# A two-layer mixer and MoE decoder: layer change interleaved, last sum kept in PSUM, branch hints near the branch

## The chip, the core and the metric

The kernel runs as one program on one core of a Trainium2 chip. The metric is device time of one execution in microseconds. Engines are named as in the profile: PE is TensorE (PEld its weight loads), DVE VectorE, ACT ScalarE, POOL GpSimd, SP the engine whose queue issues the transfers.

## What is computed

```python
for l in range(2):                                   # 256 tokens, width 1024
    h = layer_norm(ALPHA * h + mixer(h), ln1_g[l], ln1_b[l])
    h = layer_norm(ALPHA * h + moe(h),   ln2_g[l], ln2_b[l])

def layer_norm(x, g, b):
    mu = mean(x); var = mean((x - mu) ** 2)
    return (x - mu) * rsqrt(var + 1e-5) * g + b

def moe(h):                                          # 16 experts, top 2 of one group of 4
    for e in range(16):
        y += combine[:, e] * ((silu(h @ w1[e]) * (h @ w3[e])) @ w2[e])   # 1024 -> 512 -> 1024
```

The mixer begins with one wide projection of `h`, whose columns feed three attention branches.

## The kernel before

Every weight streams from HBM once, in pieces of 1 MB, over SP's queue into a ring of tiles (`ST`, issues at L96 and L100). A tile goes back to the ring when its last matmul is done, and the next piece is issued into it. float32 products of the mixer are made from two halves: ACT rounds a tile (`whi`, L370), DVE subtracts to get the rest (`wlo`, L371), and PE multiplies high by high, low by high and high by low (L375 to L377).

**MoE.** Eight pairs of experts p follow each other in an order written by hand (`block` ties each step on PE to the step before). `up` (L1557) multiplies the gathered tokens by w1 and w3, `down` (L1600) by w2. `down`'s 128x512 results are split by ACT into `yh` (L1609) and by DVE into `yl` (L1610), and `combine` adds them, weighted and scattered back to the tokens, into four accumulators in PSUM, which stay open over all eight pairs (`z` in layer 0 at L1515, `ya` in layer 1 at L1520). After p = 3 stands a branch (`overflow`, L1453): experts with more than 64 tokens would be finished in a loop. The inputs give none, so every engine jumps over that code; in the program's order it lies between p = 3 and p = 4. Each engine takes this branch on its own. A hint for it exists for PE alone, and lies right at the start of the program and right behind the first branch.

**Layer change.** The second norm of layer 0 is not finished before layer 1's first projection (the q columns) begins. `finish` (L1528) adds the residual to the accumulators (`zf`, L1539), `raw_split` (L297 on ACT, L298 on DVE) splits each eighth of it into high and low, and PE multiplies these raw sums by q's weights (L964); mean and scale are put right later. The first half of q's weight is split at L949 (ACT) and L950 (DVE) into `gl`. `norm` transposes `zf` on PE (L934), takes the statistics on DVE (L935), scales into `r`, and PE transposes `r` (L319) for the second projection (`kv`).

**End.** In layer 1 `finish` adds the residual to `ya` and writes the sum back to SBUF (`r`, L1532), then takes statistics from it (L1533). For the last pair's second column half (`down(7)`, c = 1) the work goes in two parts of 256 columns, and the last weight piece is loaded in two halves to suit. The last norm runs on DVE in two steps for each of three 512-column pieces (L1673: minus mean, times gain; L1674: times scale, plus bias), and for two 256-column pieces on ACT (L1667) and POOL (L1669, L1670). Each piece goes out by a transfer of its own (L1675).

Of the kernel before, what the change touches and what calls it, by code (L numbers as in the profile page):

```python
# [9 lines left out]
F32 = mybir.dt.float32  # L10
F32R = mybir.dt.float32r
# [58 lines left out]
def trunk(ctx, tc, x, consts, pcol, rowv, gb, wfm, wng, wdv, wmla, wcmp, wcmp2, wu, wbr, wout, rw, mw1, mw3, mw2, out):  # L70
# [223 lines left out]
    def raw_split(ps, i, k, z):  # L294
        g = ln_cols(i, k)[0]
        hi, lo = [v[:, 0:S] for v in z[k]]
        X0["z", k] = A.activation(hi, ps, AF.Copy, scale=g).ins  # L297
        V.scalar_tensor_tensor(lo, ps, g, hi.bitcast(F32), op0=ALU.mult, op1=ALU.subtract)  # L298

    def raw_fix(rs, nbs, psp, bc):  # L300
# [42 lines left out]
    def mixer(l, res, z, zf):  # L343
# [577 lines left out]

        def norm():
            r, i = res, 2 * l
            pool, tag = ST.take()
            if zf is None:
                rs, nbs, X["norm"] = ln_norm2(r, [ln_stats(r, t) for t in range(2)])
            else:
                zt = [[p.tile([P, 512], F32, name=n) for c in range(2)] for p, n in ((pO, "o"), (pS, "s"))]
                sts = [sm.tile([P, 2, 6], F32, name="lnst") for t in range(2)]
                for c in range(2):  # L930
                    for t in range(2):
                        for k in range(4):
                            with tc.issue_after(X["raw", 0, 0]):
                                T.transpose(zt[t][c][:, k * P:k * P + P], zf[:, 4 * c + k, t * P:t * P + P], ident)  # L934
                        V.bn_stats(sts[t][:, c], zt[t][c])  # L935
                rs, nbs, X["norm"] = ln_norm2(r, sts, zt)
            bc = pool.tile([P, 2048], F32, name="bc", tag=tag)
            psps = [(pT, "pt"), (pT, "pt"), (pO, "o"), (pO, "o"), (pS, "s")]
            xT[:] = ln_split_T(r, i, X["evq"], psps, *(ST.take() if zf is None else X0["zf"]))
            with tc.issue_after(X["evq"]):  # L940
                raw_fix(rs, nbs, pS, bc)
            return bc
# [1 line left out]
        add_fm("kv", xT, 4, ev1)  # L944
        add_tm("ng", xT, 280, ev2)
        w = wtile("q", 0, KD, 256)
        gl = mg.tile([P, 2, 4, 256], F32R, name="gl", tag="gt0")
        with tc.issue_after(X0["z", 1 if "yh" in X0 else 3]):
            i = A.copy(gl[:, 0], w[:, 0:4])  # L949
        V.tensor_sub(gl[:, 1], w[:, 0:4], gl[:, 0].bitcast(F32))  # L950
        with tc.issue_after(i.ins):
            w0 = [(gl[:, 0], gl[:, 1]), split(w[:, 4:8], [P, 4, 256], mb, OHL[1][1])]
        with tc.issue_after(i.ins):
            for c in fq[2:4]:
                c.h = c.prep()
            gbt = load_gb(mh, 2 * l, "gt1", nc.scalar)
# [377 lines left out]
    def moe(l, R):  # L1334
# [164 lines left out]
        def wg(*key):  # L1499
            key = (l,) + key  # L1500
            return ST.get(key), lambda: ST.done(key)
# [25 lines left out]
        def finish(c, ks):  # L1527
            if last:  # L1528
                for t in range(2):
                    a, b = ks[0] * P, ks[1] * P  # L1530
                    d = res[:, t, 512 * c + a:512 * c + b]
                    V.scalar_tensor_tensor(d, d, ALPHA, ya[t][c][:, a:b], op0=ALU.mult, op1=ALU.add)  # L1532
                    V.bn_stats(sts[t][:, c + ks[0] // 2], d)  # L1533
                return
            if c == 0:
                Z["z"] = raw_tiles(2 + 2 * l)
            for j in range(2 * c + ks[0] // 2, 2 * c + ks[1] // 2):
                d = Z["zf"][:, 2 * j:2 * j + 2]
                X0["zf", j] = V.tensor_add(d, ya[j], d).ins  # L1539
            for k in range(4 * c + ks[0], 4 * c + ks[1]):  # L1540
                raw_split(Z["zf"][:, k], 2 + 2 * l, k, Z["z"])

# [45 lines left out]
        def down(p):  # L1588
            gT = gTs[p]
            Y[p] = []  # L1590
            for c in range(2):
                parts = ((0, 2), (2, 4)) if (p, c) == (7, 1) else ((0, 4),)
                ye = [pf.tile([P, (b - a) * P], F32, name="pt") for a, b in parts]
                for h in range(2):
                    w2t, fin = wg("w2", 2 * p + c, h)
                    for v, ks in zip(ye, parts):
                        for f in range(2):
                            for j in range(2):
                                c0 = (2 * f + j) * 512
                                i = T.matmul(v[64 * j:64 * j + 64], gT[:, 2 * h + f, 64 * j:64 * j + 64],  # L1600
                                             w2t[:, c0 + ks[0] * P:c0 + ks[1] * P],
                                             start=(h == 0 and f == 0), stop=(h == 1 and f == 1), skip_group_check=True)
                    fin()
                yh = gp.tile([P, 512], F32R, name="yh")
                yl = gp.tile([P, 512], F32R, name="yl")
                Y[p].append((yh, yl))
                for v, ks in zip(ye, parts):
                    d = slice(ks[0] * P, ks[1] * P)
                    X0["yh"] = A.copy(yh[:, d], v).ins  # L1609
                    V.tensor_sub(yl[:, d], v, yh[:, d].bitcast(F32))  # L1610
                for ks in parts if p == 7 else ():
                    combine(7, c, ks)
                    finish(c, ks)
            return i

        for p in range(8):
            hs = [pf.tile([P, FF], F32, name="pt") for _ in range(2)]
            for nm, hh in zip(("w1", "w3"), hs):
                block(up, p, nm, hh)
            if p == 0:  # L1620
                lent.close()
                mx.append(right.enter_context(tc.tile_pool(name="mx2", bufs=1, side="right", reuse_waits="tile")))
                gp = right.enter_context(tc.tile_pool(name="gp", bufs=2, side="right", reuse_waits="tile"))
                block(slot_weights, 0)
            g = hidden(p, *hs)
            if p in (0, 4):
                block(gather, p // 2 + 1)
                block(slot_weights, p // 2 + 1)
                block(slots_T, p)
                block(turn, p, g)  # L1630
                if p == 4 and last:
                    affine()
                continue
            block(down, p - 1)
            block(turn, p, g)
            block(slots_T, p)
            if p == 2:
                block(gather, 2)
                block(slot_weights, 2)
            if p == 7 and not last:  # L1640
                pool, tag = X0["zf"] = ST.take()
                Z["zf"] = pool.tile([P, KD, S], F32, name="zf", tag=tag)
                for k in range(KD):
                    block(residual, k)
            for c in range(2):
                block(combine, p - 1, c)
            if p == 3:
                tc.mark_branch_hint_location('ov', 'LikelyTaken', engines=[mybir.EngineType.PE])
            if p in (3, 7):
                block(down, p)  # L1650
            if p == 3:
                for c in range(2):
                    block(combine, 3, c)
                overflow()
                PEQ.clear()
        r = res if last else hp.tile([P, 2, D], F32, name="r", tag="r")
        if last:
            gbt = [mx[b].tile([P, D], F32, name="gb", tag=f"xe{b}") for b in (2, 0)]
            for j, v in enumerate(gbt):
                nc.sync.dma_start(v, bass.AP(tensor=gb.tensor, offset=gb.offset + (4 + 4 * l + j) * D, ap=[[0, P], [1, D]]))  # L1660
            mr, nbs, ins = ln_mr2(sts)
            for t, a, b in ((1, 512, 768), (1, 768, 1024), (0, 0, 512), (0, 512, 1024), (1, 0, 512)):
                mu, rs = mr[t]
                d = r[:, t, a:b]
                g, bb = [v[:, a:b] for v in gbt]
                if b - a < 512:
                    A.activation(d, d, AF.Identity, bias=nbs[t], scale=rs)  # L1667
                    with tc.issue_after(i) if a > 512 else nullcontext():
                        G.tensor_mul(d, d, g)  # L1669
                    i = G.tensor_add(d, d, bb).ins  # L1670
                else:
                    with tc.issue_after(ins):
                        V.scalar_tensor_tensor(d, d, mu, g, op0=ALU.subtract, op1=ALU.mult)  # L1673
                    ins = V.scalar_tensor_tensor(d, d, rs, bb, op0=ALU.mult, op1=ALU.add).ins  # L1674
                nc.sync.dma_start(out[t * P:(t + 1) * P, a:b], d)  # L1675
        right.close()
        RBS.close()
# [153 lines left out]
```

## Time and profile before

| what | value |
|---|---|
| median of 3 runs | 1046.31 us (1044.56, 1046.31, 1046.35) |
| profiled execution | 1044.16 us |
| its span, first to last instruction | 1042.5 us |
| mean granted TensorE clock | 0.989 |
| PE busy | 1005.7 us (96%) |
| DVE, ACT, POOL busy | 533.7, 423.7, 31.7 us |
| bytes moved | 294.88 MB, 283 GB/s on average |

The span is what the trace shows; 1.7 us lie outside it. All times in the rows are microseconds from the span's start. PE is busy nearly all the time, so a gain has to come from the places where it waits or runs at a low clock.

### The profile page before, as it was taken

The numbers are of one execution on the slowest core, as the hardware profiler recorded it, in microseconds if no ns is written. First come the engines' busy times: TensorE is split into PE (matmuls) and PEld (weight loads), VectorE is DVE, ScalarE is ACT, GpSimd is POOL, SyncE is SP. The second block draws the span as 40 slices with busy tenths as digits, with TensorE's granted clock in tenths as the row PEclk, the third lists the DMA queues.
The fourth block names the chain that finished last, engine by engine and source line by source line (L and its number), as shares of the span: only waits on it lengthen the run. The fifth ranks groups of instructions, "written<-read, shape, count | busy, mean of one in ns | idle before, by whom it ended". The sixth has DMA issues, their size and how long they took to land. (4 is left out here: it accounts for less than half of the span.)

```text
span 1042.5 us, 16792 instructions
## 1 busy us (share of the span) xinstructions
PE 1005.7 (96%) x6498; PEld 707.3 (68%) x6498; DVE 533.7 (51%) x1493; ACT 423.7 (41%) x991; POOL 31.7 (3%) x46
## 2 busy tenths in 40 slices
PE   8999999999989999999899999999999999989994
PEld 7888888999864344433597888799998544424332
DVE  7755778785772121211395558777777422102315
ACT  6564677564432121211455547755553221101110
POOL 0300000000000000000001001000000000000001
PEclk8999999999999999999999999999999999999998
DMA  9664334548867999999955544345497789999993
GB/s 358 250 243 137 138 122 164 182 141 345 321 258 302 422 420 420 420 421 420 389 182 215 188 152 155 130 146 177 158 374 300 290 321 422 421 418 421 420 421 133
DMA packets 45543, 294.88 MB, mean 283 GB/s; under 512 B 5136, under 2 KB 7952, under 8 KB 11792
## 3 DMA queue, kind: packets, MB, share of 16 engines
q1 hardware_dynamic: 44880, 291.51, 71.3%
q10 hardware_dynamic: 576, 2.24, 0.5%
q8 instruction: 51, 0.84, 0.3%
q14 instruction: 36, 0.29, 0.1%
HBM read 292.68 MB, written 1.05 MB: 282 GB/s over the span
## 5 line engine op out<-in xcount | busy, mean ns | idle before, releaser
L1557 PE MATMUL pt<-wt,xe 128*64 128x512 f32 x1024 | 226.3, 598 | 5.3 <-DVEq L1453 4.7
L371 DVE TENSOR_TENSOR wlo<-wt,whi 128x1024 fp32r<-128x1024 f32 (+4 forms) x146 | 167.4, 1148 | 81.9 <-ACT whi L370 75.7
L370 ACT CAST whi<-wt 128x1024 fp32r<-128x1024 f32 (+4 forms) x146 | 143.8, 987 | 147.1 <-PE acc L376 103.5
L1557 PEld LDWEIGHTS pt<-wt,xe 128*64 128x64 f32 x1024 | 72.9, 138 | 143.9 <-issue 133.7
L375 PE MATMUL acc<-hi,whi 128*128 128x256 f32 x576 | 165.4, 289 | 1.7 <-ACT whi L370 0.8
L377 PE MATMUL acc<-hi,wlo 128*128 128x256 f32 x576 | 164.0, 286 | 0.8 <-DVE wlo L371 0.8
L376 PE MATMUL acc<-lo,whi 128*128 128x256 f32 x576 | 162.3, 282 | 0.0
L1600 PE MATMUL pt<-wt,gT 128*64 128x512 f32 (+1 forms) x544 | 113.9, 568 | 0.0
L375 PEld LDWEIGHTS acc<-hi,whi 128*128 128x128 f32 x576 | 108.1, 188 | 7.9 <-issue 3.9
L377 PEld LDWEIGHTS acc<-hi,wlo 128*128 128x128 f32 x576 | 108.3, 188 | 4.2 <-DVE wlo L371 2.1
L376 PEld LDWEIGHTS acc<-lo,whi 128*128 128x128 f32 x576 | 108.7, 189 | 0.3 <-DVE lo L339 0.2
L1609 ACT CAST yh<-pt 128x512 fp32r<-128x512 f32 (+1 forms) x34 | 19.1, 560 | 184.2 <-PE pt L1600 184.2
L1600 PEld LDWEIGHTS pt<-wt,gT 128*64 128x64 f32 x544 | 38.7, 137 | 70.6 <-issue 65.8
L1610 DVE TENSOR_TENSOR yl<-pt,yh 128x512 fp32r<-128x512 f32 (+1 forms) x34 | 22.4, 659 | 106.0 <-ACT yh L1609 106.0
L1568 DVE SCALAR_TENSOR_TENSOR g<-g,pt 128x512 f32<-128x512 f32 x16 | 11.0, 686 | 126.6 <-ACT g L1567 126.6
L1567 ACT ACTIVATE g<-pt 128x512 f32<-128x512 f32 x16 | 9.6, 597 | 120.4 <-PE pt L1557 120.4
L375 PE MATMUL acc<-ob,whi 128*128 128x256 f32 x192 | 56.8, 296 | 1.1 <-DVE gt L892 0.8
L376 PE MATMUL acc<-ob,whi 128*128 128x256 f32 x192 | 54.2, 282 | 0.0
L377 PE MATMUL acc<-ob,wlo 128*128 128x256 f32 x192 | 54.2, 284 | 0.0
L1569 DVE SCALAR_TENSOR_TENSOR g<-g,wsl,pt 128x512 f32<-128x512 f32 x16 | 11.9, 746 | 69.0 <-PE pt L1557 69.0
L659 DVE COPY ts<-pt 128x384 f32<-128x384 f32 x56 | 30.5, 551 | 30.7 <-PE pt L628 30.6
L1382 ACT ACTIVATE xe<-pt,pc 128x128 f32<-128x128 f32 x60 | 24.2, 453 | 53.3 <-PE pt L1324 51.6
(399 smaller groups left out, 1763.1 us busy)
## 6 DMA issues: line engine op xcount, KB each, us to landing
wt<-in_mw SPq DMA_DIRECT2D x190, 1024.0 KB, 16.8
wt<-in_wfm SPq DMA_DIRECT2D x38, 1024.0 KB, 4.9
wt<-in_wbr SPq DMA_DIRECT2D x12, 1024.0 KB, 4.8
wt<-in_wcmp SPq DMA_DIRECT2D x8, 1024.0 KB, 6.2
wt<-in_wout SPq DMA_DIRECT2D x8, 1024.0 KB, 8.1
wt<-in_wdv SPq DMA_DIRECT2D x4, 1024.0 KB, 6.2
wt<-in_wmla SPq DMA_DIRECT2D x4, 832.0 KB, 5.8
wt<-in_wng SPq DMA_DIRECT2D x4, 560.0 KB, 12.8
```

What stands on the lines that cost most here:

```text
L370: X["hi"] = A.copy(hi, src).ins
L371: X["lo"] = V.tensor_sub(lo, src, hi.bitcast(F32)).ins
L375: T.matmul(ps, a[0], b[0], start=start, stop=False)
L376: T.matmul(ps, a[0], b[1], start=False, stop=False)
L377: return T.matmul(ps, a[1], b[0], start=False, stop=stop)
L659: X["ts"] = V.tensor_copy(ts, pt).ins
L1382: A.activation(x[:, k], pj, AF.Identity, bias=bb, scale=g)
L1557: i = T.matmul(hh[64 * j:64 * j + 64], xe[p][:, 2 * h + k, j * CAP:(j + 1) * CAP], wt[:, c0:c0 + FF], start=(h == 0 and k == 0), stop=(h = ...
L1569: V.scalar_tensor_tensor(g, g, wsl[:, p:p + 1], h3, op0=ALU.mult, op1=ALU.mult)
L1600: i = T.matmul(v[64 * j:64 * j + 64], gT[:, 2 * h + f, 64 * j:64 * j + 64], w2t[:, c0 + ks[0] * P:c0 + ks[1] * P], start=(h == 0 and f == ...
L1609: X0["yh"] = A.copy(yh[:, d], v).ins
L1610: V.tensor_sub(yl[:, d], v, yh[:, d].bitcast(F32))
```

## The change

**Layer change.** The first half of the next q weight is split (`wq`) while layer 0's last pair is still being multiplied, into a ring tile that is later reused for `bc`. The orders of the residual sums, of the splits and of the weight casts are tied to it. In both layers `down(7)` c = 1 is now made part by part: part 0, then `combine(7, 0)`, then part 1, then `combine(7, 1)` in two parts.

**End.** The residual sum of the last layer stays in the accumulators: `finish` writes it into `ya` in PSUM, the statistics and the last norm's first step read it there.

**Branch hints.** The hint for PE moves to a place some 16 matmuls ahead of each branch, and DVE and ACT get hints of their own, before both branches.

```diff
@@ raw_split
-        X0["z", k] = A.activation(hi, ps, AF.Copy, scale=g).ins
+        with tc.issue_after(X0["wi"]) if i else nullcontext():
+            X0["z", k] = A.activation(hi, ps, AF.Copy, scale=g).ins
...
@@ first weight of the mixer
-        gl = mg.tile([P, 2, 4, 256], F32R, name="gl", tag="gt0")
-        with tc.issue_after(X0["z", 1 if "yh" in X0 else 3]):
-            i = A.copy(gl[:, 0], w[:, 0:4])
-        V.tensor_sub(gl[:, 1], w[:, 0:4], gl[:, 0].bitcast(F32))
...
+            w0 = [X0["w0"]]
+            i = X0["z", 4]
+        with tc.issue_after(i):
+            w0.append(split(w[:, 4:8], [P, 4, 256], mb, OHL[1][1]))
...
@@ finish
-                    d = res[:, t, 512 * c + a:512 * c + b]
-                    V.scalar_tensor_tensor(d, d, ALPHA, ya[t][c][:, a:b], op0=ALU.mult, op1=ALU.add)
-                    V.bn_stats(sts[t][:, c + ks[0] // 2], d)
+                    d, v = res[:, t, 512 * c + a:512 * c + b], ya[t][c][:, a:b]
+                    V.scalar_tensor_tensor(v, d, ALPHA, v, op0=ALU.mult, op1=ALU.add)
+                    V.bn_stats(sts[t][:, c + ks[0] // 2], v)
...
@@ down
+                    if p == 7 and (c or n):
+                        with tc.issue_after(i.ins):
+                            i = combine(7, 0 if n == 0 else 1, (0, 4) if n == 0 else (0, 2))
+                        finish(0 if n == 0 else 1, (0, 4) if n == 0 else (0, 2))
+            if p == 7:
+                with tc.issue_after(i.ins):
+                    i = combine(7, 1, (2, 4))
+                finish(1, (2, 4))
...
@@ p == 7, layer 0
+                pool, tag = X0["wq"] = ST.take()
+                wq = pool.tile([P, 2, 4, 256], F32R, name="wq", tag=tag)
...
+                X0["wi"] = A.copy(wq[:, 0], w).ins
+                X0["wl"] = V.tensor_sub(wq[:, 1], w, wq[:, 0].bitcast(F32)).ins
...
@@ before the branch
-                tc.mark_branch_hint_location('ov', 'LikelyTaken', engines=[mybir.EngineType.PE])
+                for e, at in (("PE", PEQ[-1]), ("DVE", X0["yl"]), ("Activation", X0["yh"])):
+                    with tc.issue_after(at):
+                        tc.mark_branch_hint_location("ov", "LikelyTaken", engines=[getattr(mybir.EngineType, e)])
...
@@ last norm
-                        V.scalar_tensor_tensor(d, d, mu, g, op0=ALU.subtract, op1=ALU.mult)
-                    ins = V.scalar_tensor_tensor(d, d, rs, bb, op0=ALU.mult, op1=ALU.add).ins
+                        V.scalar_tensor_tensor(v, v, mu, g, op0=ALU.subtract, op1=ALU.mult)
+                    ins = V.scalar_tensor_tensor(d, v, rs, bb, op0=ALU.mult, op1=ALU.add).ins
```

On DVE, at the first branch, before:

```order
L1610 TENSOR_TENSOR yl<-pt,yh 128x512 x2
L1331 TENSOR_TENSOR SS<-C,rks 128x256 x2
L1610 TENSOR_TENSOR yl<-pt,yh 128x512 x2
L1452 TENSOR_LOAD mxi
L1453 COMPARE_AND_BRANCH
```

and with the change:

```order
L1618 TENSOR_TENSOR yl<-pt,yh 128x512 x2
L1848 BRANCH_PREFETCH_HINT
L1337 TENSOR_TENSOR SS<-C,rks 128x256 x2
L1618 TENSOR_TENSOR yl<-pt,yh 128x512 x2
L1458 TENSOR_LOAD mxi
L1459 COMPARE_AND_BRANCH
```

One hint stands between the two pairs of `yl`, the second pair and one load ahead of the branch; the second layer has the same rows.

On PE at the layer change, before: `gl` is the split first half of q's weight, `whi` and `wlo` the second, L934 the transposes of `norm`.

```order
L964 MATMUL acc<-z,gl 128x258 x24
L964 MATMUL acc<-z,whi 128x258 x2
L934 MATMUL o<-idb,zf 128x128 x4
L934 MATMUL s<-idb,zf 128x128 x4
L934 MATMUL o<-idb,zf 128x128 x4
L934 MATMUL s<-idb,zf 128x128 x4
L964 MATMUL acc<-z,whi 128x258 x14
L964 MATMUL acc<-z,wlo 128x258 x8
```

With the change (`wq` for `gl`, L970 for L964, L935 for L934):

```order
L970 MATMUL acc<-z,wq 128x258 x24
L970 MATMUL acc<-z,whi 128x258 x10
L935 MATMUL o<-idb,zf 128x128
L970 MATMUL acc<-z,whi 128x258 x6
L970 MATMUL acc<-z,wlo 128x258 x8
L935 MATMUL o<-idb,zf 128x128 x3
L935 MATMUL s<-idb,zf 128x128 x4
L935 MATMUL o<-idb,zf 128x128 x4
L935 MATMUL s<-idb,zf 128x128 x4
```

All but one of the transposes have moved behind the raw products. On DVE beside them five `wlo` stand ahead of the first statistics, where four stood.

On PE at the end of layer 1, before: `y_9033` and `y_9035` are the two token halves' accumulators of columns 0 to 511, `y_9034` and `y_9036` those of columns 512 to 1023.

```order
L1600 MATMUL pt<-wt,gT 64x512 x8
L1520 MATMUL y_9033<-yh,CT 128x512
L1520 MATMUL y_9035<-yh,CT 128x512
L1520 MATMUL y_9033<-yl,CT 128x512
L1520 MATMUL y_9035<-yl,CT 128x512
L1600 MATMUL pt<-wt,gT 64x256 x16
L1520 MATMUL y_9034<-yh,CT 128x256
L1520 MATMUL y_9036<-yh,CT 128x256
L1520 MATMUL y_9034<-yl,CT 128x256
L1520 MATMUL y_9036<-yl,CT 128x256
```

With the change the first two are called `y_9035` and `y_9037`, the others `y_9036` and `y_9038`:

```order
L1611 MATMUL pt<-wt,gT 64x512 x8
L1611 MATMUL pt<-wt,gT 64x256 x8
L1526 MATMUL y_9035<-yh,CT 128x512
L1526 MATMUL y_9035<-yl,CT 128x512
L1526 MATMUL y_9037<-yh,CT 128x512
L1526 MATMUL y_9037<-yl,CT 128x512
L1611 MATMUL pt<-wt,gT 64x256 x8
L1526 MATMUL y_9036<-yh,CT 128x256
L1526 MATMUL y_9038<-yh,CT 128x256
L1526 MATMUL y_9036<-yl,CT 128x256
L1526 MATMUL y_9038<-yl,CT 128x256
```

The four `combine` instructions of columns 0 to 511 have moved from ahead of the 16 part products to between the two parts. SP's and POOL's instructions stand in the same order as before.

## Rows read from the trace of the kernel before

**Rows 1.** The page: span, and GB/s moved in 40 slices

```profile
span 1042.5 us, 16792 instructions
GB/s 358 250 243 137 138 122 164 182 141 345 321 258 302 422 420 420 420 421 420 389 182 215 188 152 155 130 146 177 158 374 300 290 321 422 421 418 421 420 421 133
```

**Rows 2.** Line L1453 on DVE: ns min/median/max; first and last start

```profile
L1453 DVEq COMPARE_BRANCH  x2: 63/68/72, 411.1 to 920.9; - x2
L1453 DVEq EVENT_SEMAPHORE  x2: 21/21/21, 411.7 to 926.6; - x2
```

**Rows 3.** Timeline of PE behind the two branches; start, us, idle before in brackets

```profile
412.72 7.52 PE L1557 MATMUL pt<-wt,xe 128*64 128x512 f32 x34 [0.48 <-PEq L1453]
...
926.64 15.65 PE L1557 MATMUL pt<-wt,xe 128*64 128x512 f32 x64 [4.65 <-DVEq L1453]
```

**Rows 4.** Chain of waits in layer 1: two of the `up` blocks

```profile
926.64 15.65 PE pt L1557 x64
...
947.25 13.88 PE pt L1557 x64
```

**Rows 5.** Stretches of layer 1: us; busy by engine; PEclk; DMA share; GB/s

```profile
848.00:921.00 73.00, 72.98 (x359) 30.63 (x356) 13.68 (x28) 11.68 (x24) 0.00 (x0) 1.00 1.01 421
921.00:927.00 6.00, 1.35 (x6) 0.50 (x6) 0.20 (x1) 0.00 (x0) 0.00 (x0) 1.00 1.02 415
927.12:930.53 3.41, 3.41 (x11) 0.97 (x9) 0.00 (x0) 0.00 (x0) 0.00 (x0) 0.50 1.02 418
```

**Rows 6.** PE in `down(6)`; a weight issue with its us to landing

```profile
1007.81 7.21 PE L1600 MATMUL pt<-wt,gT 128*64 128x512 f32 x32
...
993.22 0.33 SPq L100 DMA_DIRECT2D wt<-in_mw  x1
...
wt<-in_mw SPq DMA_DIRECT2D x1, 1024.0 KB, 19.8
```

**Rows 7.** Timeline of PE at the layer change

```profile
517.55 1.87 PE L964 MATMUL acc<-z,gl 128*128 128x258 f32 x10 [0.97 <-ACT gl L949]
...
521.20 3.33 PE L964 MATMUL acc<-z,gl 128*128 128x258 f32 x14 [1.79 <-DVE z L298]
...
535.53 0.38 PE L319 MATMUL pt<-idb,r 128*128 128x128 f32 x2
...
538.23 0.50 PE L375 MATMUL acc<-hi,whi 128*128 128x256 f32 x2
```

**Rows 8.** Timeline of DVE at the layer change

```profile
521.46 2.35 DVE L371 TENSOR_TENSOR wlo<-wt,whi 128x1024 fp32r<-128x1024 f32 x2
...
526.45 0.69 DVE L935 BATCH_NORM_STATS2 lnst<-o 128x6 f32<-128x512 f32 x1
...
533.13 0.99 DVE L271 TENSOR_SCALAR r<-s,lnmv,rqy 128x256 f32<-128x256 f32 x2
```

**Rows 9.** Stretches of the layer change, columns as in rows 5

```profile
517.52:520.93 3.41, 1.86 (x10) 1.37 (x10) 3.41 (x5) 3.41 (x5) 0.00 (x0) 1.00 0.82 336
520.93:524.35 3.42, 3.15 (x14) 3.15 (x15) 3.42 (x6) 2.76 (x6) 0.00 (x0) 0.50 0.77 249
```

**Rows 10.** Timeline of PE and DVE at the end

```profile
1021.96 0.73 PE L1520 MATMUL y<-yh,CT 128*128 128x512 f32 x2 [0.69 <-ACT yh L1609]
...
1023.22 1.28 DVE L1532 SCALAR_TENSOR_TENSOR r<-r,y 128x512 f32<-128x512 f32 x2 [0.59 <-PE y L1520]
...
1030.58 0.35 DVE L254 BATCH_NORM_AGGREGATE lnmv<-lnst 128x2 f32<-128x18 f32 x2
```

**Rows 11.** Lines of the last norm, and one with a PSUM operand

```profile
L1673 DVE SCALAR_TENSOR_TENSOR r<-r,lnmv,gb x3: 746/1204/1206, 1032.8 to 1037.0; 128x512 f32<-128x512 f32 x3
...
L1674 DVE SCALAR_TENSOR_TENSOR r<-r,rqy,gb x3: 751/1094/1286, 1033.6 to 1038.3; 128x512 f32<-128x512 f32 x3
...
L1669 POOL TENSOR_TENSOR r<-r,gb x2: 722/944/1167, 1033.6 to 1035.4; 128x256 f32<-128x256 f32 x2
...
L1568 DVE SCALAR_TENSOR_TENSOR g<-g,pt x16: 677/687/690, 322.7 to 1001.8; 128x512 f32<-128x512 f32 x16
```

More of the change, by code (lines that the diff above doesn't have):

```diff
@@ L923, in norm @@
             r, i = res, 2 * l
-            pool, tag = ST.take()
+            pool, tag = ST.take() if zf is None else X0["wq"]
             if zf is None:
@@ L946, in mixer @@
         w = wtile("q", 0, KD, 256)
-        gl = mg.tile([P, 2, 4, 256], F32R, name="gl", tag="gt0")
-        with tc.issue_after(X0["z", 1 if "yh" in X0 else 3]):
-            i = A.copy(gl[:, 0], w[:, 0:4])
-        V.tensor_sub(gl[:, 1], w[:, 0:4], gl[:, 0].bitcast(F32))
-        with tc.issue_after(i.ins):
-            w0 = [(gl[:, 0], gl[:, 1]), split(w[:, 4:8], [P, 4, 256], mb, OHL[1][1])]
-        with tc.issue_after(i.ins):
+        if zf is None:
+            gl = mg.tile([P, 2, 4, 256], F32R, name="gl", tag="gt0")
+            with tc.issue_after(X0["z", 3]):
+                i = A.copy(gl[:, 0], w[:, 0:4]).ins
+            V.tensor_sub(gl[:, 1], w[:, 0:4], gl[:, 0].bitcast(F32))
+            w0 = [(gl[:, 0], gl[:, 1])]
+        else:
+            w0 = [X0["w0"]]
+            i = X0["z", 4]
+        with tc.issue_after(i):
+            w0.append(split(w[:, 4:8], [P, 4, 256], mb, OHL[1][1]))
+        with tc.issue_after(i if zf is None else X0["z", 7]):
             for c in fq[2:4]:
@@ L1538, in finish @@
                 d = Z["zf"][:, 2 * j:2 * j + 2]
-                X0["zf", j] = V.tensor_add(d, ya[j], d).ins
+                with tc.issue_after(X0["wl"]):
+                    X0["zf", j] = V.tensor_add(d, ya[j], d).ins
             for k in range(4 * c + ks[0], 4 * c + ks[1]):
@@ L1592, in down @@
                 parts = ((0, 2), (2, 4)) if (p, c) == (7, 1) else ((0, 4),)
[L1593 to L1603, printed above, removed]
+                w2 = [wg("w2", 2 * p + c, h) for h in range(2)]
                 yh = gp.tile([P, 512], F32R, name="yh")
@@ L1606, in down @@
                 Y[p].append((yh, yl))
-                for v, ks in zip(ye, parts):
+                for n, ks in enumerate(parts):
+                    v = pf.tile([P, (ks[1] - ks[0]) * P], F32, name="pt")
+                    with tc.issue_after(i.ins) if p == 7 and (c or n) else nullcontext():
+                        for h in range(2):
+                            for f in range(2):
+                                for j in range(2):
+                                    c0 = (2 * f + j) * 512
+                                    i = T.matmul(v[64 * j:64 * j + 64], gT[:, 2 * h + f, 64 * j:64 * j + 64],
+                                                 w2[h][0][:, c0 + ks[0] * P:c0 + ks[1] * P],
+                                                 start=(h == 0 and f == 0), stop=(h == 1 and f == 1), skip_group_check=True)
+                            if ks[1] == 4:
+                                w2[h][1]()
                     d = slice(ks[0] * P, ks[1] * P)
                     X0["yh"] = A.copy(yh[:, d], v).ins
[L1610 to L1613, printed above, removed]
+                    X0["yl"] = V.tensor_sub(yl[:, d], v, yh[:, d].bitcast(F32)).ins
+                    if p == 7 and (c or n):
[6 more added lines that the diff above has]
+                finish(1, (2, 4))
             return i
@@ L1642, in moe @@
                 Z["zf"] = pool.tile([P, KD, S], F32, name="zf", tag=tag)
+                pool, tag = X0["wq"] = ST.take()
+                wq = pool.tile([P, 2, 4, 256], F32R, name="wq", tag=tag)
+                w = ST.get((l + 1, "q", 0))[:, 0:1024].rearrange("p (k c) -> p k c", k=4)
+                X0["wi"] = A.copy(wq[:, 0], w).ins
+                X0["wl"] = V.tensor_sub(wq[:, 1], w, wq[:, 0].bitcast(F32)).ins
+                X0["w0"] = (wq[:, 0], wq[:, 1])
                 for k in range(KD):
@@ L1663, in moe @@
                 mu, rs = mr[t]
-                d = r[:, t, a:b]
+                d, v = r[:, t, a:b], ya[t][a // 512][:, a % 512:(b - 1) % 512 + 1]
                 g, bb = [v[:, a:b] for v in gbt]
                 if b - a < 512:
-                    A.activation(d, d, AF.Identity, bias=nbs[t], scale=rs)
+                    A.activation(d, v, AF.Identity, bias=nbs[t], scale=rs)
                     with tc.issue_after(i) if a > 512 else nullcontext():
```

## The prediction

> **What bounds the kernel now.** I read the page first: PE is busy 96% of a span of 1042.5 us, and the bytes moved stand at 420 GB/s in two long stretches, one in each layer's MoE [rows 1]. So two limits are near each other, and every place has to be asked which of them ends last there. Then I looked for what PE waits for. The chain of waits and PE's timeline give four places that the change touches.
>
> The branch. DVE takes it at 411.1 us in layer 0 and goes on at 411.7; in layer 1 it takes it at 920.9 and goes on at 926.6 [rows 2]. The same instruction costs 0.6 us once and 5.7 us the other time. PE waits 0.48 us behind the first and 4.65 us, 'DVEq', behind the second [rows 3]. The wait has a tail: just behind it PE runs at a granted clock of 0.50, its lower level, for 3.41 us [rows 5], and the `up` block there takes 15.65 us where the next takes 13.88 [rows 4]. The profile puts the wait down to the branch by both names, and the 1.77 us on top come with the low clock that follows an idle PE.
>
> The transfers beside it. From 848 us on the transfer engines are full: share 1.01 and 421 GB/s over 73 us, and 415 GB/s during the stall itself [rows 5]. What that means shows at `down(6)`: its fourth piece of w2 is issued at 993.22 and lands 19.8 us later, at 1013.0. `down(6)` starts at 1007.81 and gives each of its four pieces 8 of its 32 matmuls in 7.21 us, so it wants that piece at 1007.81 + 3/4 of 7.0 = 1013.1 [rows 6]. The weight is 0.1 us ahead of its use. PE after its stall has just been caught by the stream.
>
> The layer change. PE waits 0.97 us for ACT's cast of `gl` and 1.79 us for DVE's low half of z [rows 7]. Between the two it is busy 1.86 of 3.41 us, and the next stretch runs at a clock of 0.50 [rows 9]. The end is ordered by DVE and POOL: statistics done at 1030.58 [rows 10], then the last norm.
>
> **The change, part by part.**
>
> *Hints.* For DVE the hint stands about 3 us ahead of the branch. If it works, 5.66 us of DVE's stall shrink to about the 0.6 us of layer 0, and PE regains 4.17 us of waiting (4.65 less the 0.48 of layer 0) and 1.77 us of clock: 5.94 us. But PE meets the stream 86 us later. The stream was full throughout the stall, so its landings cannot come earlier by what PE saves; PE would wait at `down(6)` and behind it for what it saved at the branch. What is left is what the stream itself lost there: 415 and 418 GB/s against 421 for some 9 us are 0.1 us, and up to 0.6 us if pieces are issued a little sooner. I take 0.3 us. In layer 0 there is 0.48 us to win at most; I count it as nothing.
>
> *Layer change.* The split moves under the last pair's products, where DVE and ACT have room (its weight has landed by then). PE's wait of 0.97 us goes: the raw products can start at 516.6, when the last `combine` is done. What bounds next? DVE's work ahead of the statistics is the same amount, with one `wlo` more and `gl` gone (both about 1.2 us; two `wlo` are 2.35 us [rows 8]). It starts earlier, because part 0 of `down(7)` is summed while part 1 is multiplied. Laying the instructions out with their durations, I get the first statistics at 525.6 instead of 526.45. From there to the last piece of `r` DVE needs what it needed before, 533.13 + 0.99 - 526.45 = 7.7 us [rows 8], so 533.3.
>
> PE's work up to the transposes of `r`: before, 535.53 - 517.55 = 18.0 us, of which 1.79 are waiting and half of 3.15 are the low clock [rows 7, 9], so 14.6 us of products. From 516.6 on these end at 531.2. PE is then no longer the last: it waits for `r`, whose first transposes can go at about 532.7, 2.8 us before the 535.53 of now. The later ones wait for the last pieces, which takes 0.4 us back. So the first `kv` product comes 2.4 us before 538.23. Between here and the full stream PE sets the pace, so all later issues shift with it, and the stream's end too. Bounds: 0.5 us if only part of the 0.97 us is kept; 3.2 us if nothing waits for `r`. `wq` takes a ring tile earlier than `bc` did; the transfers have room there (share 0.82 and 0.77 [rows 9]), so I count that as nothing.
>
> *Order at the end.* Before, `combine(7, 0)` runs while the last pieces land, and its two sums and two statistics on DVE (1.28 + about 1.28 us from 1023.22 on [rows 10]) lie under PE's part products. With the change they come behind part 0, which needs the second last landing, so they start about 2 us later, and DVE still has them when part 1 is ready. Statistics and sum now also use the same accumulator, so the last `combine` waits for the statistics ahead of it. Laid out with the old landings the statistics are done 0.65 us later than now; if the weights lay ready 0.65 us sooner. I take 0.5 us of loss, with bounds of -0.2 and +1.0.
>
> *Last norm.* Its six DVE instructions take 746/1204/1206 and 751/1094/1286 ns, 6.3 us in all; the short ones are those with no POOL instruction beside them [rows 11]. The first operand now lies in PSUM. A row of this form without POOL is L1568, 687 ns, about 0.65 apart [rows 11]. No row shows the form beside POOL. Bounds: if POOL slows it as before, nothing is gained (I leave 0.3 us); if not, six of 0.65 are 3.9 us and POOL's chain of four ends last, at 722 ns each instead of up to 1167, some 2.2 us before now. I take 2.0 us, since the slow ones among the rows have both large operands in SBUF. [...]
>
> *The sum.* -0.3 - 2.4 + 0.5 - 2.0 = -4.2 us. From the profiled execution's own 1044.16 that is 1040.0. That execution is the fastest of four; the runs lie in two groups, near 1044.4 and near 1046.3, and the median is of the upper. By the upper group the result would be 1042.1. I take 1041.4.
>
> **Rivals.**
>
> 1. *The stream is not the limit.* Then the branch gives all its 5.9 us and the end order 0.65 instead of -0.5: -2.4 - 5.9 - 0.65 - 2.0 = -11, so 1033.2 to 1035.3. For it: the stall is plain in PE's rows. Against it: the 0.1 us of slack and the share of 1.01. It would need a stream that can run above 421 GB/s, which it does nowhere in the page's 40 slices by more than 1.
>
> 2. *No change to speak of.* The wait for `r` lies at 530 to 532.7, behind a busy PE; if the granted clock falls behind it, as it did behind the 1.79 us, 3.4 us at 0.50 take back some 1.5 us. With a POOL that still slows DVE the total is -0.3 - 0.9 + 0.5 - 0.3 = -1.0 us: 1043.2 to 1045.3.
>
> 3. *Slower: layer 0's branch falls into the long case.* The two branches run the same code and cost 0.6 and 5.7 us, so the cost depends on where the code lies, and every instruction added shifts it. If the hint does not help and the target of layer 0 now has to be fetched, that costs up to 5.9 us, and nothing covers it: the stream of layer 0 can't give it back, it is PE's own time. Total -4.2 + 5.9 = +1.7 us, slower by more than 0.2% once the other gains come to under 3.8 us: 1045.9 to 1048.5. [...]
>
> **How the numbers follow.** My forecast has 0.62, rival 1 0.08, rival 2 0.18, rival 3 0.12. A measurement of this kernel can tell about 0.2%, 2.1 us, from no change. The forecast and rival 1 are faster: 0.70. Rival 2 and the weaker part of rival 3 are the same: 0.22. Slower: 0.08. The forecast's own bounds add up to gains of 0.2 less than nothing and 6.2 at most, so 1038.0 to 1046.5 over both groups of runs. For 8 in 10 I give 1036.5 to 1045.0: it leaves out rival 1's far end, the weakest corner of the forecast and rival 3.
>
> **What the new profile would show.** Hints: DVE's wait in L1453's rows about 0.6 us in both layers, no clock of 0.50 behind the second, and PE waits that name transfers from `down(6)` on, with landings as dense as before. If PE doesn't wait there, rival 1 is right. Layer change: no wait on `wq`, the first raw product at about 516.6, a wait of some 2 us for `r`, and `kv` 2.4 us sooner; a clock of 0.50 there is rival 2. End: statistics at most 1 us later against the last landing, and the last norm's DVE rows near 0.69 us beside POOL. The prediction is wrong if DVE's slow rows stay, if layer 0's branch takes longer than 1 us, or if PE finds its weights landed after a branch without a stall.

## The result, and the profile after

The changed kernel takes 1040.23 us (median of 6 runs, 1037.63 to 1040.66) against 1045.98 us before in the same measurement: 0.9946 of the time before, with an interval of 0.9935 to 0.9956. That is 5.7 us less; the prediction had 4.2 us less and 1041.4 us. The profiled execution took 1040.32 us.

```profile
span 1038.6 us, 16795 instructions
```

The branch comes first, since the prediction said most of it. The rows are those of its line on DVE (ns min/median/max, then first and last start), then PE's timeline behind the two branches:

```profile
L1459 DVEq COMPARE_BRANCH  x2: 74/79/84, 413.0 to 918.5; - x2
L1459 DVEq EVENT_SEMAPHORE  x2: 21/21/21, 413.6 to 924.2; - x2
```

```profile
414.49 5.80 PE L1564 MATMUL pt<-wt,xe 128*64 128x512 f32 x26 [0.43 <-PEq L1459]
...
924.28 16.14 PE L1564 MATMUL pt<-wt,xe 128*64 128x512 f32 x64 [4.76 <-DVEq L1459]
```

Against [rows 2, 3] nothing has changed: DVE still goes on 5.7 us after it takes the branch of layer 1, PE still waits 4.76 us for it, and the `up` block behind takes 16.14 us (15.65 [rows 4]). The hint, which was to shrink this, has not.

The layer change, on ACT, DVE and PE (start, us, idle before in brackets):

```profile
511.66 0.59 ACT L1617 CAST yh<-pt 128x512 fp32r<-128x512 f32 x1 [4.94 <-PE pt L1611]
512.14 1.05 ACT L1659 CAST wq<-wt 128x1024 fp32r<-128x1024 f32 x1
...
518.15 0.38 PE L1521 MATMUL z<-CT,yl 128*128 128x256 f32 x1 [0.92 <-DVE yl L1618]
...
526.66 0.69 DVE L936 BATCH_NORM_STATS2 lnst<-o 128x6 f32<-128x512 f32 x1
...
532.24 0.54 DVE L271 TENSOR_SCALAR r<-o,lnmv,rqy 128x256 f32<-128x256 f32 x1
...
518.61 3.03 PE L970 MATMUL acc<-z,wq 128*128 128x258 f32 x24
...
532.83 0.96 PE L320 MATMUL pt<-idb,r 128*128 128x128 f32 x4 [0.73 <-DVE lnnb L260]
...
536.05 0.48 PE L376 MATMUL acc<-hi,whi 128*128 128x256 f32 x2
```

The first `yh` of `down(7)` on ACT is a good mark to count from, since nothing ahead of it was changed but the hints. Before, the same row and the start of the last `down(7)` in layer 1 were:

```profile
509.89 0.59 ACT L1609 CAST yh<-pt 128x512 fp32r<-128x512 f32 x1 [4.94 <-PE pt L1600]
...
1017.62 3.65 PE L1600 MATMUL pt<-wt,gT 128*64 128x512 f32 x16
```

From `yh` to the first `kv` product it was 538.23 - 509.89 = 28.34 us [rows 7], and is now 536.05 - 511.66 = 24.39. The cast of `wq` starts right behind `yh`, and no row shows the waits of 0.97 and 1.79 us any more. In their place PE waits 0.92 us for `yl` of the second part (518.15), just ahead of the first raw products, and 0.73 us for `r` (532.83; the row names `lnnb`, which DVE computes right behind the first piece of `r`). The first raw product comes 6.95 us after `yh` (518.61) against 7.66 before.

The end, on PE and DVE, and then the lines of the last norm:

```profile
1015.71 4.57 PE L1611 MATMUL pt<-wt,gT 128*64 128x512 f32 x24
1020.44 1.08 PE L1611 MATMUL pt<-wt,gT 128*64 128x256 f32 x8 [0.17 <-DMA wt<-in_mw]
...
1026.70 0.36 PE L1526 MATMUL y<-yh,CT 128*128 128x256 f32 x1 [1.49 <-DVE lnst L1539]
...
1028.55 0.35 DVE L254 BATCH_NORM_AGGREGATE lnmv<-lnst 128x2 f32<-128x18 f32 x2
```

```profile
L1694 DVE SCALAR_TENSOR_TENSOR y<-y,lnmv,gb x3: 748/750/753, 1030.7 to 1033.7; 128x512 f32<-128x512 f32 x3
...
L1695 DVE SCALAR_TENSOR_TENSOR r<-y,rqy,gb x3: 749/751/751, 1031.5 to 1034.4; 128x512 f32<-128x512 f32 x3
...
L1690 POOL TENSOR_TENSOR r<-r,gb x2: 725/726/726, 1031.5 to 1033.0; 128x256 f32<-128x256 f32 x2
```

From the start of `down(7)` to the statistics done it was 1030.58 - 1017.62 = 12.96 us [rows 10], and is 12.84. In the last norm DVE's six steps all take 750 ns and POOL's 726, where they took up to 1286 and 1167 [rows 11]: POOL no longer slows DVE, nor DVE POOL.

One thing disturbs the comparison of the two profiled executions. `yh` comes at 511.66, 1.77 us later than before, though nothing ahead of it was changed but the hints. Two stretches of layer 0 differ (us; busy of PE, PEld, DVE, ACT, POOL; PEclk; DMA share; GB/s), after and then before:

```profile
163.00:167.00 4.00, 3.50 (x16) 3.29 (x17) 4.00 (x18) 3.00 (x13) 0.00 (x0) 0.64 0.59 215
297.00:301.00 4.00, 4.00 (x16) 4.00 (x17) 3.59 (x22) 2.15 (x4) 0.00 (x0) 0.57 0.57 197
```

```profile
163.00:167.00 4.00, 3.19 (x24) 2.99 (x25) 4.00 (x18) 3.00 (x13) 0.00 (x0) 1.00 0.63 225
297.00:301.00 4.00, 3.75 (x26) 3.64 (x25) 3.74 (x25) 2.15 (x4) 0.00 (x0) 1.00 0.75 272
```

PE's granted clock was 0.64 and 0.57 there, and 1.00 before. These are averages: in quarters of a microsecond it reads 1.00 up to 297.25 us, 0.50 from 297.5 to 300.5 and 1.00 again from 300.75. In another execution of the changed kernel (the last run below) it is 1.00 in both stretches, `yh` comes at 509.71, and the time is 1038.31 us. But the kernel without the branch has 1.00 in both too, and its `yh` comes at 511.63: these stretches are not the whole cause, and the rest stays open. Counted from `yh` on, the two profiled executions differ by 3.95 (layer change), -0.27 (from `kv` to `down(7)`), 0.12 (to the statistics) and 1.80 us (from the statistics' end to DVE's last step, 8.44 and 6.64): 5.6 us, close to the 5.7 between the medians.

### The profile page after: what moved, and what is told of

Same layout as the page of the kernel before. It is cut to its first block, busy times and chain, and to the rows that moved or that the text cites. A ratio compares the mean times of both kernels' runs of the same rounds, so it can differ in the third digit from the quotient of the medians.

```text
span 1038.6 us, 16795 instructions
## 1 busy us (share of the span) xinstructions
PE 1006.2 (97%) x6498; PEld 708.3 (68%) x6498; DVE 532.0 (51%) x1493; ACT 424.0 (41%) x991; POOL 30.7 (3%) x46
```

## The experiments

**Hints alone.** The kernel before, with only this:

```diff
-                tc.mark_branch_hint_location('ov', 'LikelyTaken', engines=[mybir.EngineType.PE])
+                for e, at in (("PE", PEQ[-1]), ("DVE", X0["yl"]), ("Activation", X0["yh"])):
+                    with tc.issue_after(at):
+                        tc.mark_branch_hint_location("ov", "LikelyTaken", engines=[getattr(mybir.EngineType, e)])
```

> The kernel before with the branch hints of the change and nothing else. My theory now, from the profile after: the hint on VectorE does nothing; its wait at the branch of layer 1 stays at 5.7 us, PE's wait there at 4.7 us, and the time stays within 1 us of the kernel before. Rival (what I had forecast): the wait falls to 0.6 us, and the time by 0.3 us if the weight stream takes up the rest, by 5.9 us if it does not.

Measured: 0.9998 of the time before (0.9989 to 1.0006). DVE's rows at the branch:

```profile
L1453 DVEq COMPARE_BRANCH  x2: 74/79/84, 410.7 to 920.3; - x2
L1453 DVEq EVENT_SEMAPHORE  x2: 21/21/21, 411.3 to 925.8; - x2
```

The wait is 5.5 us. The hints do nothing that can be measured. What they fetch shows in the changed kernel's transfers at the first hints, from 400 to 412 us (queues: packets, MB, share):

```profile
q1 hardware_dynamic: 688, 5.00, 100.3%
q8 instruction: 1, 0.02, 0.6%
```

PE's hint lies at 403.3, about 10 us ahead of the branch (all of `down(3)` and more lie between, not only some 16 matmuls), and at 408.2 a block of code comes over the first instruction queue (q8), which was not there before. I take that block to be PE's, since this queue brings one for some 250 of PE's instructions all through the trace (53 blocks for 12996 matmuls and weight loads). There was little to win by it: PE's own wait behind layer 0's branch is 0.48 us before [rows 3] and 0.43 in the changed kernel. The second instruction queue (q14), on which blocks come behind the branch (one from 414 to 416 us, two from 918.5 to 924.2), is not in the list: nothing was fetched over it at the hints of DVE and ACT.

**The hint nearer.** DVE's hint stood 10 us ahead of the branch, so it might have come too early.

```diff
                 block(down, p)
+                if p == 3:
+                    with tc.issue_after(X0["yl"]):
+                        tc.mark_branch_hint_location("ov", "LikelyTaken", engines=[mybir.EngineType.DVE])
```

> The changed kernel with VectorE's hint moved to right behind the last yl before the branch, 0.5 us ahead of it in place of 10 us. My theory: the hint on VectorE fetches nothing wherever it stands, and the wait at the branch of layer 1 stays above 5 us. Rival: at 10 us ahead what was fetched is gone again by the time of the branch; nearer, the wait shrinks by the time it has been under way.

Measured, in one profiled execution: the wait is 5.8 us.

```profile
L1459 DVEq COMPARE_BRANCH  x2: 74/79/84, 411.3 to 916.6; - x2
L1459 DVEq EVENT_SEMAPHORE  x2: 21/21/21, 412.0 to 922.4; - x2
```

**DVE's code moved by 64 instructions.** The padding is the hint itself, of which a single one had changed nothing.

```diff
-                for e, at in (("PE", PEQ[-1]), ("DVE", X0["yl"]), ("Activation", X0["yh"])):
+                for e, at in (("PE", PEQ[-1]),) + (("DVE", X0["yl"]),) * (65 if last else 1) + (("Activation", X0["yh"]),):
```

> The changed kernel with the hint for VectorE of layer 1 given 65 times over in place of once, which moves VectorE's branch of layer 1 and all behind it by 64 instructions and leaves every order as it is. My theory: the long wait depends on where the branch and its target lie in VectorE's code, so it falls from 5.7 us to 0.6 us as in layer 0, and the time by 0.5 us or less, since the weight stream takes up the rest. Rival 1: the wait stays, being a matter of layer 1's traffic. Rival 2: the wait goes and the time falls by 5 us.

Measured: 0.9941 (0.9928 to 0.9954), the changed kernel within its interval. The branch's rows, the transfers at the padding, and PE behind the branch:

```profile
L1459 DVEq COMPARE_BRANCH  x2: 74/79/84, 411.0 to 916.5; - x2
L1459 DVEq EVENT_SEMAPHORE  x2: 21/21/21, 411.6 to 917.0; - x2
```

```profile
q1 hardware_dynamic: 200, 1.47, 99.5%
...
q14 instruction: 1, 0.01, 0.6%
```

```profile
917.99 13.95 PE L1564 MATMUL pt<-wt,xe 128*64 128x512 f32 x64 [0.44 <-PEq L1459]
...
993.09 1.94 PE L1564 MATMUL pt<-wt,xe 128*64 128x512 f32 x8 [0.46 <-DMA wt<-in_mw]
...
1000.64 1.94 PE L1611 MATMUL pt<-wt,gT 128*64 128x512 f32 x8 [0.65 <-DMA wt<-in_mw]
...
1008.01 1.94 PE L1611 MATMUL pt<-wt,gT 128*64 128x512 f32 x8 [0.56 <-DMA wt<-in_mw]
...
1016.87 1.08 PE L1611 MATMUL pt<-wt,gT 128*64 128x256 f32 x8 [0.67 <-DMA wt<-in_mw]
```

The wait in layer 1 is 0.56 us, and PE's is 0.44. During the padding (906.4 to 911.2 us) a block of code comes over the second instruction queue, which in the changed kernel shows no packet in the same stretch. What shortened the wait this run does not separate. My theory is that it hangs on where the branch and its target lie in DVE's code; layer 0's branch, of 0.6 us without any hint on DVE, speaks for it. But the padding is 65 hints for this very branch, and the block comes at 910.8, 4.4 us behind the first of them, much as PE's block came 4.9 us behind its hint: that the repeated hint fetched it is not excluded. Padding of another kind was not run.

The time did not fall. PE waits 4.3 us less at the branch, and begins to wait for weights at 993, some 0.5 us for each piece. There are seven such waits up to 1008, of which three are shown, and the one ahead of part 0.

**No branch at all.** The hints and `overflow()` are left out.

> The changed kernel without the branch, its hints and the overflow code behind it (no expert overflows with these inputs, so only that code is left out). PE's wait of 4.7 us and the low clock behind it are gone. My theory: the weight stream sets the end, PE waits for weights later, and the time falls by 0.5 us or less. Rival: PE sets the end, and the time falls by 5 to 6 us (to about 0.989 of the kernel before).

Measured: 0.9944 (0.9932 to 0.9957), the changed kernel again. PE's waits are for weights from 1003 on:

```profile
1002.98 1.94 PE L1611 MATMUL pt<-wt,gT 128*64 128x512 f32 x8 [0.36 <-DMA wt<-in_mw]
...
1010.35 1.94 PE L1611 MATMUL pt<-wt,gT 128*64 128x512 f32 x8 [0.54 <-DMA wt<-in_mw]
```

How little the stall was worth shows from `yh` to the first product of the last `combine`, here and then in the padded kernel:

```profile
511.63 0.59 ACT L1617 CAST yh<-pt 128x512 fp32r<-128x512 f32 x1 [4.94 <-PE pt L1611]
...
1026.85 0.35 PE L1526 MATMUL y<-yh,CT 128*128 128x256 f32 x1 [1.49 <-DVE lnst L1539]
```

```profile
509.64 0.59 ACT L1617 CAST yh<-pt 128x512 fp32r<-128x512 f32 x1 [4.94 <-PE pt L1611]
...
1024.50 0.36 PE L1526 MATMUL y<-yh,CT 128*128 128x256 f32 x1 [1.49 <-DVE lnst L1539]
```

That is 515.22 us without the branch and 514.86 padded, against 515.04 (1026.70 - 511.66) and 514.93 in two executions of the changed kernel, which has the stall.

**The layer change alone.** The changed kernel with the old hint, the old order of `down(7)` in the last layer and the old `finish` and last norm (the diffs are those of the change, undone).

> The changed kernel with the old hints, the old order of down(7) in the last layer and the old last norm, so that the layer change alone is left. My theory now: the layer change is worth 4.1 us, and that is the time gained (1042 against 1046). Rival: it is worth the 2.4 us of the prediction, and the other 1.7 us of the gain came from elsewhere.

Measured: 0.9962 (0.9949 to 0.9976), some 4.0 us less than before; the medians, 1041.89 and 1044.87 us, are 3.0 us apart. From `yh` to `kv`:

```profile
510.81 0.59 ACT L1642 CAST yh<-pt 128x512 fp32r<-128x512 f32 x1 [4.92 <-PE pt L1636]
...
535.21 0.48 PE L376 MATMUL acc<-hi,whi 128*128 128x256 f32 x2
```

This is 24.40 us, as in every run with the whole layer change (24.39 to 24.42), against 28.34, 28.48 and 28.37 in the three without it.

**The early split without the new order.** As the last, but with the old order of `down(7)` in layer 0 too (`if last and p == 7` becomes `if p == 7`).

> The layer change alone with the early split of q's weight, but the old order of down(7) and combine(7) in both layers. The mark is the time from the first yh of down(7) in layer 0 to the first kv product: 28.3 us before, 24.4 us with the change. My theory: split and order share the gain, and it comes to about 26 us. Rival: the early split is all of it, 24.4 us.

Measured, in one profiled execution: 537.34 - 510.81 = 26.53 us.

```profile
510.81 0.59 ACT L1617 CAST yh<-pt 128x512 fp32r<-128x512 f32 x1 [4.94 <-PE pt L1608]
...
515.81 0.69 DVE L1546 TENSOR_TENSOR zf<-z,zf 128x512 f32<-128x512 f32 x1 [1.57 <-PE z L1521]
...
537.34 0.48 PE L376 MATMUL acc<-hi,whi 128*128 128x256 f32 x2
```

The early split gives 1.8 us, and the new order on top of it 2.1 us. Where the second comes from shows on DVE: between the first `yl` and the first piece of `r` it stands idle for 2.3 us here, 1.57 of them for `combine`, and for 0.6 us in the changed kernel, with as many `wlo` to do in both. No run has the new order without the split.

**The end alone.** The kernel before, with `finish` and the last norm of the change.

> The kernel before with the residual sum left in PSUM and the last norm reading it there, and the old order. My theory: the six steps of the last norm take 0.75 us each beside POOL and the time falls by 1.8 us. [...]

Measured: 0.9989 (0.9980 to 0.9998), 1.2 us less. The last norm took 6.65 us against 8.44, 1.8 us less, but the statistics come later. PE and DVE:

```profile
1018.36 3.65 PE L1600 MATMUL pt<-wt,gT 128*64 128x512 f32 x16
...
1029.92 0.36 PE L1520 MATMUL y<-yh,CT 128*128 128x256 f32 x1 [1.49 <-DVE lnst L1533]
...
1031.77 0.35 DVE L254 BATCH_NORM_AGGREGATE lnmv<-lnst 128x2 f32<-128x18 f32 x2
```

From `down(7)` to the statistics it is 13.41 us, 0.45 more than the 12.96 of before. PE waits 1.49 us for a statistics instruction: it now reads the accumulator in PSUM that the last products are to go to.

**The old order at the end of the changed kernel.** `down(7)` in the last layer as in the kernel before.

> The changed kernel, but with the old order of down(7) and combine(7) in the last layer (the layer change keeps the new one). My theory: the new order costs 0.8 us there, so this kernel is 0.8 us faster than the changed one (6.4 us under the kernel before), and the statistics end 6.0 us behind the last landing instead of 6.75. Rival: the last landing sets the end in either order, and the time is that of the changed kernel.

Measured: 0.9944 (0.9931 to 0.9958), no faster than the changed kernel. `down(7)` to statistics: 1028.04 - 1014.62 = 13.42 us, against 12.84. My theory falls: the new order does not cost 0.8 us, it saves 0.6 in these two executions. How much it saves depends on the stream: in two more executions with the changed kernel's end (the hint nearer, and the changed kernel once more) the stretch takes 12.40 us, where PE waits for no weights in it, and 12.99, where it waits 0.30 us ahead of part 0 (0.17 in the first). I had compared with the last landing, and PE did not wait for that one.

**Half of the sums in SBUF.**

```diff
-                    V.scalar_tensor_tensor(v, d, ALPHA, v, op0=ALU.mult, op1=ALU.add)
-                    V.bn_stats(sts[t][:, c + ks[0] // 2], v)
+                    s = d if c else v
+                    V.scalar_tensor_tensor(s, d, ALPHA, v, op0=ALU.mult, op1=ALU.add)
+                    V.bn_stats(sts[t][:, c + ks[0] // 2], s)
...
-            for t, a, b in ((1, 512, 768), (1, 768, 1024), (0, 0, 512), (0, 512, 1024), (1, 0, 512)):
+            for t, a, b in ((1, 512, 768), (1, 768, 1024), (0, 512, 1024), (0, 0, 512), (1, 0, 512)):
```

> The changed kernel with the residual sums of columns 512 to 1023 written to SBUF as before (those of columns 0 to 511 stay in PSUM), and the last norm beginning with that piece of the first token half, while POOL is still idle. My theory: what the change lost at the end is PE's wait for statistics in the same accumulator, not the new order; the statistics end 6.0 us behind the last landing instead of 6.75, the last norm keeps its 6.6 us, and the kernel is 0.7 us faster than the changed one. Rival: the new order is what costs, and nothing changes (6.7 us).

Measured: 0.9926 (0.9913 to 0.9938). The last norm takes 6.65 us, as expected, and PE's wait falls to 0.49 us. But the statistics end 6.28 us behind the last landing, not 6.0, and 12.88 us behind the start of `down(7)`, as in the changed kernel: PE now waits for the stream (0.27 and 0.22 us) in its stead. The time lies under the changed kernel's, but the intervals overlap, and none of the three stretches in the table below is shorter for it.

**Both put together, and the changed kernel once more.**

> The layer change of the changed kernel, its hints, the old order of down(7) and combine(7) in the last layer, and the sums of columns 512 to 1023 in SBUF as in e8_half_sbuf: of the end only the sums of columns 0 to 511 in PSUM and the last norm's steps are left. My theory: the statistics end 6.0 us behind the last landing, the last norm keeps 6.65 us, and from the last landing to the end it takes 12.65 us against 13.4 in the changed kernel, so it is about 0.7 us faster than that. Rival: with the stream setting the end, order and place cost nothing, and it equals the changed kernel.

> The changed kernel once more, on the same chip as e10_best, to compare the two. Both theories: 5.7 us under the kernel before, within 1 us.

Measured in one measurement: 1039.68 us, 0.9940 (0.9927 to 0.9953), and 1039.67 us, 0.9947 (0.9934 to 0.9960). They are equal, and the expected 0.7 us is not there. PE and DVE of the first:

```profile
1015.42 3.65 PE L1609 MATMUL pt<-wt,gT 128*64 128x512 f32 x16
...
1025.98 0.35 PE L1526 MATMUL y<-yh,CT 128*128 128x256 f32 x1 [0.49 <-DVE r L1539]
...
1028.39 0.36 DVE L254 BATCH_NORM_AGGREGATE lnmv<-lnst 128x2 f32<-128x18 f32 x2
```

12.97 us from `down(7)` to the statistics: with the old order and the wait of 0.49 us it is the 12.96 us of before. No version of these beats the changed kernel beyond its interval.

| kernel | `yh` to `kv` | `down(7)` to statistics | statistics to last step |
|---|---|---|---|
| before | 28.34 | 12.96 | 8.44 |
| changed | 24.39 | 12.84 | 6.64 |
| changed, once more | 24.42 | 12.99 | 6.65 |
| changed, hint nearer | 24.41 | 12.40 | 6.65 |
| end alone (old order, PSUM) | 28.37 | 13.41 | 6.65 |
| changed, old order at the end | 24.40 | 13.42 | 6.65 |
| half in SBUF, new order | 24.41 | 12.88 | 6.65 |
| half in SBUF, old order | 24.42 | 12.97 | 6.65 |

## Why the prediction came out as it did

**Hints: -0.3 us forecast, nothing measured, and the reason was wrong.** The step that failed is 'if it works, 5.66 us of DVE's stall shrink to about the 0.6 us of layer 0'. A single hint fetched nothing for DVE, at 10 us ahead (I had reckoned 3) or at 0.5, and the wait stayed between 5.5 and 5.8 us. That the number came out nearly right is luck as far as the hint goes; it rests on the next step, which the padded kernel and the one without a branch bear out: the stream was full (421 GB/s and a share of 1.01 from 930 to 1000 us in both), and with the wait really gone PE gave its time back to weights, piece by piece, 0.36 to 0.65 us in the rows shown up to 1011 us. (The slack of 0.1 us at `down(6)` is 0.2 when three quarters of the 7.21 us in the row are taken, which changes nothing.) Rival 1, that the branch is worth 5.9 us, is refuted by these two and not by the changed kernel, in which the wait was never removed.

**Layer change: -2.4 us forecast, -3.95 measured.** The mechanism was right, the size was off at two places. The first statistics came 526.66 - 511.66 = 15.00 us after `yh` against 16.56 before, 1.56 us sooner where I had 0.85. And PE's transposes of `r` began 6.17 us behind the first statistics, as soon as its first piece was there (532.24 + 0.54), where I had 7.1; before it was 9.08, since PE came to them late [rows 7, 8]. The 7.1 was too much by the trace of before already: DVE began the first piece of `r` 5.71 us behind the first statistics (526.45 [rows 8]), and one piece is about half of this row, 6.2 us in all:

```profile
532.16 0.99 DVE L271 TENSOR_SCALAR r<-o,lnmv,rqy 128x256 f32<-128x256 f32 x2
```

The wait for `r` was 0.73 us and not some 2, and no low clock followed it: the granted clock is 1.00 from 532 to 540 us. Rival 2 did not come about.

**Order at the end: +0.5 us forecast, -0.1 measured.** The term was two effects of opposite sign, and I had let the wrong one prevail. The new order saves 0.6 us (12.84 against 13.42; 0.4 to 1.0 over three executions), and the statistics in the accumulators cost 0.45 (13.41 against 12.96), by PE's longer wait for them. The forecast had the first as a loss, by the old landings; PE waited only 0.17 us for a landing here.

**Last norm: -2.0 us forecast, -1.80 measured.** POOL and DVE left each other alone, as the likelier bound had it; the choice of that bound was an estimate, since no row had the form beside POOL. The steps take 750 ns and not 687: the nearest row was the line's own shortest, 746. And DVE still ends last, at 1035.19, and not POOL's chain, which is done at 1034.52. With a PSUM operand the steps take 748 to 753 ns beside POOL, what they took without one and without POOL (746 and 751 [rows 11]). The slow ones of before, 1094 to 1286 ns [rows 11], had both large operands in SBUF; now one of the two lies in PSUM.

**Rival 3.** Layer 0's branch took 0.6 us in every run that has it. Its reason, that the cost depends on where the code lies, is not shown: the padded kernel fits it, but doesn't separate place from repeated hints. (By its own sum the upper end of its range is 1048.0 and not 1048.5.)

**The sum.** From mark to mark the gain is 5.6 us where 4.2 were forecast: 1.55 more at the layer change and 0.6 more by the order at the end, 0.2 less in the last norm, 0.3 less by the hints, and 0.3 lost between `kv` and `down(7)`. Measured against the medians, the time of 1040.2 us lies inside the range, a little under the 1041.4 that I took.

## What to carry to other kernels

A stall on an engine that runs just behind a full stream can be worth nothing, as the 4.76 us were here beside 415 GB/s (515.22 and 514.86 us from mark to mark without it, 515.04 and 514.93 with it), and this is proved only by really removing it: see whether waits for the stream come up behind it in its stead, as the seven of some 0.5 us did here. Between stages, give the first weights' preparation to engines that idle under the last products of the stage before (1.8 us here), and then ask again which engine ends last; half of the gain at the layer change (2.1 us) came from the new order, which let that engine, DVE, begin earlier. And when an operand moves to PSUM to save one engine from another, look who else wants that accumulator: here PE, which waited 1.49 us for it where it had waited 0.49.

## What the runs showed that I had not expected

A branch on DVE takes 0.6 or 5.7 us in the same kernel, and 64 more hints ahead of it turned the one into the other; whether by moving its code or by being hints is open. A hint on PE was followed by a block of code 4.9 us later, a single one on DVE by none. The granted clock of unchanged stretches differs from execution to execution (1.00 or 0.57 from 297 to 301 us), and `yh` lies anywhere between 509.1 and 511.8 us in these runs, only in part for that reason; a gain of a few us is better read from a mark behind such stretches than from the time.
